# Splitting w_o beside the last products instead of in the chunk stage, in a pool + SSD decoder step

## The chip, the core and the metric

One core of one Trainium2 chip. The metric is the device time of one launch in microseconds; lower is better. The engines are TensorE (PE, with its weight loads PEld), VectorE (DVE), ScalarE (ACT), GpSimd (POOL) and SyncE (SP, which here issues most of the DMAs; ACT issues the rest).

## The reference

One layer of a hybrid decoder, for 1024 prompt rows and 8 x 8 sample rows, in float32:

```
h = rmsnorm(x) * (1 + scale) + shift
[u_pool | z_pool | z_ssm | xBC | dt | g] = h @ w_in
P = (pool_mix(u_pool) * silu(z_pool)) @ w_pool_out
S = gated_rmsnorm(SSD(conv(xBC)) + D*x, z_ssm) @ w_ssm_out
m = sigmoid(g_pool) * P + sigmoid(g_ssm) * S
x = x + gate * (m @ w_o)          # w_o is 1024 x 1024
y = rmsnorm(x)
```

The SSD part is a scan over 8 chunks of 128 rows, for 4 groups of 8 heads. The outputs also hold the new states.

## The kernel before

Every float32 product is made of three matmuls: each operand is split into a part "hi" (a copy in a rounded format, written by ACT) and a part "lo" (value less hi, written by POOL or DVE), and hi*hi, hi*lo and lo*hi are added up in PSUM.

The stages, by the time of the profiled execution: norms and the projections by `w_in` up to about 800 us; the chunk stage (32 chunks, group by group) to about 1120 us; the last products of group 2 to 1140 us; the tail, which is the S products of group 3 with everything that makes m from them, to about 1206 us; and the final product m @ w_o with the last norm to 1297 us.

**Chunk stage.** The loop over the 32 chunks interleaves them with pieces of products (`products(t)`): the eight P units and the S units of groups 0 to 2. PE's order is the order of the code (`in_line((PE,))`). A scheduler sets the order on the other engines, and each engine then works in its order. From chunk 13 on the loop also takes two steps of `wo_splits()` per chunk. For each of 16 half row blocks of w_o (128 x 512) it loads the raw values into `pw` (L1668, SP's queue, two buffers), copies hi into `ph` on ACT (L1674, one buffer), stores hi to the DRAM tile `wo_d` from ACT's queue (L1675), subtracts lo on POOL (L1676), and stores lo from SP's queue (L1670). The steps of a chunk that the prediction speaks of: ACT computes dec (L1196), cE (L1392), bt (L1406), xw (L1415); DVE computes dec (L1416), cE (L1418), xwl (L1419) and the gate product v (L1362); PE uses them in L1208, L1211 and L1429.

**Tail.** `tail_unit(m)` for m = 0 to 7 is one S product (36 matmuls at L354 to L356 in three groups of 384, 352 and 352 columns, into a PSUM pool of three banks) and what follows it. `m_done(m)` loads the gates R (L1785) and the other half of m (L1790), makes the gains R * rstd at the unit's start (L1788, three DVE instructions out of PSUM), adds each group from PSUM to the accumulator G (L1795, DVE), multiplies by R (L1800, DVE) and adds the other half (L1801, POOL, on DVE for m = 7). `wo_prep(k)` loads hi and lo of row block k of w_o back from `wo_d` (L1761, L1762; 512 KB each). `m_split(k)` splits the accumulator: 64 sample columns as `sh` (ACT L1768, DVE L1769), 1024 prompt columns as hi and lo (ACT L1779, DVE L1780). `samples[k]` are four matmuls with the sample columns (L1774). rstd, a row of PSUM that all units use, is made by L1740 to L1749 at the start of the tail. The row blocks 5 to 7 are loaded after the units.

The final product (L1892 to L1894) needs hi and lo of all eight row blocks of w_o and of m for each block of rows.

Of the kernel before, what the change touches and what calls it, by code (L numbers as in the profile page):

```python
# [8 lines left out]
F32 = mybir.dt.float32  # L9
F32R = mybir.dt.float32r  # L10
AF = mybir.ActivationFunctionType
ALU = mybir.AluOpType
# [3 lines left out]
PRIO = 2000  # L16
# [4 lines left out]
P = 128  # L21
D = 1024
# [4 lines left out]
T = SEQ + NS  # L27
# [19 lines left out]
def tile_pool_ssd_step(  # L47
# [6 lines left out]
    nc = tc.nc  # L54
    uid = [0]

    def nm(s):
        uid[0] += 1
        return f"{s}_{uid[0]}"
# [3 lines left out]
    sm = ctx.enter_context(tc.tile_pool(name="sm", bufs=2))  # L63
# [32 lines left out]
    def PB():  # L96
        return psB.tile([P, 512], F32, tag="ps", name=nm("ps"))
# [7 lines left out]
    load = nc.sync.dma_start  # L105
    store_ = nc.scalar.dma_start
    mm = nc.tensor.matmul
    act = nc.scalar.activation
    V = nc.vector
# [77 lines left out]
    dg = []  # L187
# [146 lines left out]
    def in_line(engines, begin=False):  # L334
        traced = nc.cur_bb.bb.instructions
        for i in traced[len(traced) if begin else line[0]:]:
            if i.engine in engines:
                if i.engine in line[1]:
                    tc.add_manual_dep(i, line[1][i.engine], mybir.DependencyInfo(
                        mybir.DependencyClass.NoSync, mybir.DependencyReason.DATA), reason="in_line")  # L340
                line[1][i.engine] = i.name
        line[0] = len(traced)
# [42 lines left out]
    def dram(name, shape, dt=F32):  # L385
        return dr.tile(list(shape), dt, tag=name, name=name)
# [1084 lines left out]
    def run_units(units, ahead=1, beside=None):  # L1471
        pend = {}
        widx = [i for i, u in enumerate(units) if u[0] is not None]
        nxt = 0
        done_w = 0
        for i, (pf, run) in enumerate(units):
            if pf is not None:
                while nxt < len(widx) and nxt <= done_w + ahead:
                    pend[widx[nxt]] = units[widx[nxt]][0]()
                    nxt += 1  # L1480
                done_w += 1
                it = run(pend.pop(i))
                for _ in it or ():
                    if beside is not None:
                        beside()
            else:
                run(None)
        while later:
            step()
# [113 lines left out]
    ck = right.__enter__()  # L1603
# [54 lines left out]
                nxt += 1  # L1658
            yield from run(ws.pop(i))
    pc_ = pieces()  # L1660
    wo_d = [dram(f"wo{k}", [P, 2, D]) for k in range(8)]

    def wo_splits():
        raws = {}
        for n in range(18):
            if n < 16:
                raws[n] = ck.tile([P, 512], F32, tag="pw", name=nm("pw"), bufs=2)
                load(raws[n], w_o[0, n // 2 * P:n // 2 * P + P, n % 2 * 512:n % 2 * 512 + 512])  # L1668
            if n > 1:
                load(wo_d[(n - 2) // 2][:, 1, n % 2 * 512:n % 2 * 512 + 512], raws.pop(n - 2))  # L1670
            yield
            if n < 16:
                hi = ck.tile([P, 512], F32R, tag="ph", name=nm("ph"), bufs=1)
                act(hi, raws[n], AF.Copy)  # L1674
                store_(wo_d[n // 2][:, 0, n % 2 * 512:n % 2 * 512 + 512], hi.bitcast(F32))  # L1675
                nc.gpsimd.tensor_tensor(raws[n].bitcast(F32R), raws[n], hi.bitcast(F32), ALU.subtract)  # L1676
            yield
    wos = wo_splits()
    RATE = 2.56
    FRONT = 4  # L1680

# [11 lines left out]
        next(pc_)  # L1693
    next(seq[0])
    for i in range(len(seq)):
        if i > 12:
            next(wos, None)
        if i + 1 < len(seq):
            with behind(mybir.EngineType.DVE, 1 - i) if i < 2 else ExitStack():
                next(seq[i + 1])  # L1700
        products(i + 0.4)
        if i > 0:
            next(seq[i - 1], None)
        if i > 12:
            next(wos, None)
        next(seq[i], None)
        if i % NC == 3:
            sample_end(i // NC)
        if i + 3 < len(seq):
            next(seq[i + 3])  # L1710
        if i + 2 < len(seq):
            with behind(mybir.EngineType.Activation) if i == 0 else ExitStack():
                next(seq[i + 2])
        products(i + 1.0)
    next(seq[-1], None)
    for it in (pc_, wos):
        for _ in it:
            pass
    in_line((mybir.EngineType.PE,))
    right.__exit__(None, None, None)  # L1720
    while right_all:
# [2 lines left out]


    mp = ctx.enter_context(tc.tile_pool(name="mp", bufs=8, side="right", reuse_waits="tile"))
    mq = open_("mq", 5)

    def M(shape=(P, T), dt=F32):
        return mq.tile(list(shape), dt, tag="m", name=nm("m"))  # L1730
# [6 lines left out]
    ps = PB()  # L1737
    for c in range(9):
        n = min(P, T - c * P)
        mm(ps[:n, c:c + 1], sq_acc[:, c * P:c * P + n], ones[:, 0:1], start=True, stop=True)  # L1740
    for n, c in ((P, slice(0, 8)), (NS, slice(8, 9))):
        act(rs9[:n, c], ps[:n, c], AF.Sqrt, bias=eps[:n], scale=1.0 / DI)
        V.reciprocal(rs9[:n, c], rs9[:n, c])
    rstd = [PB() for _ in range(3)]
    for c in range(9):
        n = min(P, T - c * P)
        dg = sm.tile([P, P], F32, tag="stc", name=nm("dg"), bufs=4)[:n, :n]
        V.tensor_scalar(dg, ident[:n, :n], rs9[:n, c:c + 1], None, ALU.mult)
        mm(rstd[c // 4][:, c % 4 * P:c % 4 * P + n], ones[:n, :], dg, start=True, stop=True)  # L1749

    wo, mh, ml = [None] * 8, [None] * 8, [None] * 8
    w4 = [Y4(hp), Y4(hp)]
    pso = [PB(), PB()]
    samples = []

    def wo_prep(k, mem):
        if k < 4:
            hi, lo = w4[0][:, k, :D], w4[1][:, k, :D]
        else:
            hi, lo = mem((P, D), F32R), mem((P, D), F32R)  # L1760
        load(hi.bitcast(F32), wo_d[k][:, 0])  # L1761
        load(lo.bitcast(F32), wo_d[k][:, 1])  # L1762
        wo[k] = (hi, lo)

    def m_split(k, mem):

        sh = sm.tile([P, P], F32R, tag="stc", name=nm("sh"), bufs=4)
        act(sh[:, 0:NS], acc[k][:, SEQ:], AF.Copy)  # L1768
        V.tensor_tensor(sh[:, NS:P], acc[k][:, SEQ:], sh[:, 0:NS].bitcast(F32), ALU.subtract)  # L1769

        def sample_mm():
            for part in wo[k]:
                for half in range(2):
                    mm(pso[half], sh, part[:, half * 512:half * 512 + 512],  # L1774
                       start=(k == 0 and part is wo[k][0]), stop=(k == 7 and part is wo[k][1]))
        samples.append(sample_mm)
        hi, lo = mem((P, SEQ), F32R), mem((P, SEQ), F32R)
        for o, n in (((0, 384), (384, 384), (768, 256)) if k == 7 else ((0, SEQ),)):
            act(hi[:, o:o + n], acc[k][:, o:o + n], AF.Copy)  # L1779
            V.tensor_tensor(lo[:, o:o + n], acc[k][:, o:o + n], hi[:, o:o + n].bitcast(F32), ALU.subtract)  # L1780
        mh[k], ml[k] = hi, lo

    def m_done(m):
        r = R()
        load(r, gs_d[m])  # L1785
        for j, ps in enumerate(rstd):
            s = slice(512 * j, min(512 * j + 512, T))
            V.tensor_tensor(r[:, s], ps[:, :s.stop - s.start], r[:, s], ALU.mult)  # L1788
        mt = M()
        load(mt, m1_d[m])  # L1790
        a = acc[m]

        def done(o, n, ps):
            s = slice(o, o + n)
            V.tensor_tensor(a[:, s], ps[:, :n], a[:, s], ALU.add)  # L1795
            if m < 7:
                s = slice(0, T)
                if o + n < T:
                    return
            V.tensor_tensor(a[:, s], a[:, s], r[:, s], ALU.mult)  # L1800
            (nc.gpsimd if m < 7 else V).tensor_tensor(a[:, s], a[:, s], mt[:, s], ALU.add)  # L1801
        return done

    def tail_unit(m):
        pf, run_ = S_unit(3, m, m_done)

        def run(w):
            for _ in run_(w):
                pass
            if m < 5:  # L1810
                wo_prep(m, M)
            if m < 7:
                m_split(m, M8 if m < 4 else G)
            if m < 5:
                with tc.high_priority(PRIO):
                    samples[m]()
        return (pf, run)
    run_units([tail_unit(m) for m in range(8)])
    y4 = [Y4(hs), Y4(hs)]
    slots = [y[:, q] for y in y4 for q in range(4)]  # L1820

    def late(shape, dt=F32R):
        return slots.pop(0)[:, :shape[1]]
    for k in (5, 6):
        wo_prep(k, late)
        samples[k]()
    wo_prep(7, late)
    m_split(7, late)
    sample_mm = samples[7]

    def w2k(tag):
# [10 lines left out]
    for half in range(2):  # L1842
        c = slice(half * 512, half * 512 + 512)
# [31 lines left out]
    for i in range(8):  # L1875
# [4 lines left out]
        r = R((P, D))  # L1880
# [6 lines left out]
        for j, (c0, cw) in enumerate(cuts):  # L1887
            s = slice(c0, c0 + cw)
            ps = PB()
# [56 lines left out]
```

## Time and profile before

| | |
|---|---|
| median of 3 runs | 1298.56 us (1297.77 to 1300.59) |
| span of the profiled execution | 1297.1 us |
| PE busy | 1255.9 us, 97% |
| DVE busy | 910.5 us, 70% |
| ACT busy | 708.8 us, 55% |
| POOL busy | 677.4 us, 52% |
| DMA | 251.70 MB, 194 GB/s over the span |

The span is that of one execution under the profiler, of 26554 instructions; the other time is the median of plain runs. PE is the engine with hardly any idle time, so the end moves where PE waits. In a window row the columns are the window, its length, then busy time and number of instructions for PE, PEld, DVE, ACT and POOL, then the granted PE clock, the busy share of the DMA engines and GB/s. In a group row stand busy time, mean ns of one, and the idle time of the engine ahead of them with its releasers. In a row of waits stand who waited for whom, us in total, times, and the longest. In a timeline row stand start, duration, engine and line; in brackets the idle time before it and what ended it.

### The profile page before, as it was taken

The page shows a single profiled execution, that of the slowest core. Times are in us where ns is not written, and L with a number is a line of the kernel's source. Part 1 is how long each engine was busy: PE and PEld are TensorE (multiplying, and loading weights), DVE is VectorE, ACT ScalarE, POOL GpSimd, SP SyncE. Part 2 cuts the span into 40 slices and gives each one's busy share as a digit, 9 for nine tenths or more (in the row PEclk, how much of TensorE's full clock was granted, in tenths as well). Part 3 has the DMA queues.
Part 4 walks back from the last instruction along what each step waited for, and adds up shares of the span by engine and source line. Part 5 has one row for each costly group of instructions (what it writes and reads, how often), then busy time and mean ns, then how long its engine had stood idle before and what let it go on. Part 6 is the DMA issues. An engine that isn't in the chain of part 4 may idle for free.

```text
span 1297.1 us, 26554 instructions
## 1 busy us (share of the span) xinstructions
PE 1255.9 (97%) x9771; PEld 1173.9 (90%) x9771; DVE 910.5 (70%) x1580; ACT 708.8 (55%) x1684; POOL 677.4 (52%) x563
## 2 busy tenths in 40 slices
PE   7999999999999999999999999999998999999998
PEld 6779999989999999999889999889998999999786
DVE  4685778866979578775777665488676888576433
ACT  4665356375656564545455453687987868201111
POOL 1007668677869776664344444276776747314000
PEclk9999999999999999999999999999999999999999
DMA  9837345465455544444656555999988656575631
GB/s 326 259 107 224 119 150 173 142 202 170 146 180 197 165 155 133 161 135 129 181 158 173 152 178 164 356 355 354 338 270 262 202 168 199 172 266 159 226 106 52
DMA packets 233795, 251.70 MB, mean 194 GB/s; under 512 B 31265, under 2 KB 177905, under 8 KB 233658
## 3 DMA queue, kind: packets, MB, share of 16 engines
q1 hardware_dynamic: 161568, 171.60, 42.1%
q10 hardware_dynamic: 72098, 78.41, 17.5%
q8 instruction: 77, 1.26, 0.4%
q14 instruction: 52, 0.43, 0.1%
HBM read 167.06 MB, written 83.01 MB: 193 GB/s over the span
## 4 chain that ended last, share of the span: by engine, by line
PE 67%; issue 8%; DMA 8%; DVE 6%; POOL 5%; ACT 4%; SPq 0%; ACTq 0%; POOLq 0%; DVEq 0%
PE ps L603 6%; PE ps L604 6%; PE ps L605 6%; PE mm L603 6%; PE mm L605 6%; PE mm L604 6%; PE mm L355 3%; PE mm L356 3%; PE mm L354 3%; PE ps L1208 2%; PE ps L1892 2%; PE ps L1894 2%; PE ps L1893 2%; POOL wlo L163 2%; PE ps L1211 2%
## 5 line engine op out<-in xcount | busy, mean ns | idle before, releaser
L163 POOL TENSOR_TENSOR wlo<-rawA,whi 128x512 fp32r<-128x512 f32 x120 | 184.0, 1538 | 185.6 <-ACT whi L160 101.6
L163 POOL TENSOR_TENSOR wlo<-raw,whi 128x512 fp32r<-128x512 f32 x92 | 150.7, 1646 | 125.3 <-ACT whi L160 91.1
L354 PE MATMUL mm<-Y,whi 128*128 128x352 f32 (+1 forms) x480 | 160.1, 334 | 0.7 <-DVE G L1795 0.5
L355 PE MATMUL mm<-Y,whi 128*128 128x352 f32 (+1 forms) x480 | 157.3, 328 | 1.0 <-DVE Y L1466 1.0
L356 PE MATMUL mm<-Y,wlo 128*128 128x352 f32 (+1 forms) x480 | 156.9, 327 | 0.0
L605 PE MATMUL mm<-Y,wlo 128*128 128x272 f32 x496 | 143.6, 290 | 3.9 <-POOL wlo L163 3.1
L603 PE MATMUL ps<-Y,whi 128*128 128x272 f32 x496 | 144.5, 291 | 2.3 <-ACT o L803 1.7
L603 PE MATMUL mm<-Y,whi 128*128 128x272 f32 x496 | 146.5, 295 | 0.2
L604 PE MATMUL ps<-Y,whi 128*128 128x272 f32 x496 | 143.1, 289 | 0.0
L604 PE MATMUL mm<-Y,whi 128*128 128x272 f32 x496 | 142.9, 288 | 0.0
L605 PE MATMUL ps<-Y,wlo 128*128 128x272 f32 x496 | 142.6, 288 | 0.0
L160 ACT ACTIVATE whi<-rawA 128x512 fp32r<-128x512 f32 x125 | 78.2, 626 | 95.6 <-PE ps L604 44.9
L1051 DVE SCALAR_TENSOR_TENSOR GA<-GA,cvT,GA 128x1112 f32<-128x1112 f32 x72 | 127.1, 1769 | 0.6 <-ACT GA L1048 0.5
L160 ACT ACTIVATE whi<-raw 128x512 fp32r<-128x512 f32 x96 | 58.7, 626 | 91.4 <-DVE raw L549 41.7
L605 PEld LDWEIGHTS mm<-Y,wlo 128*128 128x128 f32 x496 | 93.4, 188 | 5.8 <-POOL wlo L163 4.2
L603 PEld LDWEIGHTS ps<-Y,whi 128*128 128x128 f32 x496 | 93.3, 188 | 4.0 <-ACT o L803 1.9
L603 PEld LDWEIGHTS mm<-Y,whi 128*128 128x128 f32 x496 | 93.3, 188 | 2.5 <-issue 0.8
L604 PEld LDWEIGHTS mm<-Y,whi 128*128 128x128 f32 x496 | 93.4, 188 | 0.7 <-issue 0.6
L604 PEld LDWEIGHTS ps<-Y,whi 128*128 128x128 f32 x496 | 93.3, 188 | 0.3 <-issue 0.2
L605 PEld LDWEIGHTS ps<-Y,wlo 128*128 128x128 f32 x496 | 93.4, 188 | 0.2 <-issue 0.2
L354 PEld LDWEIGHTS mm<-Y,whi 128*128 128x128 f32 x480 | 90.3, 188 | 3.2 <-DVE G L1795 1.4
L355 PEld LDWEIGHTS mm<-Y,whi 128*128 128x128 f32 x480 | 90.3, 188 | 3.2 <-DVE Y L1466 1.6
(452 smaller groups left out, 3851.6 us busy)
## 6 DMA issues: line engine op xcount, KB each, us to landing
rawA<-in_w_in SPq DMA_DIRECT2D x46, 512.0 KB
dec<-acs_d SPq DMA_DIRECT2D x32, 512.0 KB
xbc<-GA ACTq DMA_DIRECT2D x24, 512.0 KB
xb<-xbc SPq DMA_DIRECT2D x32, 384.0 KB
rawA<-in_w_in SPq DMA_DIRECT2D x32, 256.0 KB
pw<-in_w_ssm_out ACTq DMA_DIRECT2D x32, 256.0 KB
ws<-ph ACTq DMA_DIRECT2D x32, 256.0 KB
ws<-pw SPq DMA_DIRECT2D x32, 256.0 KB
```

The source lines that it names most:

```text
L160: ins = act(hi[:, :, :ncols], raw[:, :, :ncols], AF.Copy)
L163: (eng or nc.gpsimd).tensor_tensor(lo[:, :, :ncols], raw[:, :, :ncols], hi[:, :, :ncols].bitcast(F32), ALU.subtract)
L354: mm(ps[:, :n], a, rh[k][:, o:o + n], start=(k == 0), stop=False)
L355: mm(ps[:, :n], a, rl[k][:, o:o + n], start=False, stop=False)
L356: mm(ps[:, :n], b, rh[k][:, o:o + n], start=False, stop=(k == nk - 1))
L603: mm(p, hi, ah, start=(k == 0), stop=False)
L604: mm(p, hi, al, start=False, stop=False)
L605: mm(p, lo, ah, start=False, stop=(k == 3))
L1051: V.scalar_tensor_tensor(d[:, :n], rp[:, k:k + n], cvT[:, 24 * k + mc:24 * k + mc + 1], d[:, :n], ALU.mult, ALU.add)
L1208: mm(o[hh], xd[:S, 2 * q + hh, :], dec[:S, 2 * q + hh], start=True, stop=state is None)
L1211: mm(o[hh], state[:, h * 64:h * 64 + 64], cE[:, h], start=False, stop=True)
L1892: mm(ps[:, :cw], mhk, wo[k][0][:, s], start=(k == 0), stop=False)
```

## The change

`wo_splits()` and the DRAM tiles `wo_d` go, with the steps in the chunk loop. In the tail, `wo_load(k)` loads the raw row block k (128 x 1024, 512 KB) into a tile of the pool `mq`, and `wo_split(k)` copies hi on ACT and subtracts lo on POOL (on DVE for k = 7), in the units 0 to 5 and after them for 6 and 7. `mq` has 8 buffers instead of 5, and the nine diagonal tiles `dg` lie in one of them. In unit m the split of m - 1 and the sample matmuls of m - 2 are made. The gains are made behind the unit's adds, except for m = 7. PE and DVE follow the order of the code in the tail. The DMA scratch of the program is set to 1024.

```
-    wo_d = [dram(f"wo{k}", [P, 2, D]) for k in range(8)]
-    def wo_splits(): ...
     for i in range(len(seq)):
-        if i > 12:
-            next(wos, None)
...
-        if i > 12:
-            next(wos, None)
...
-    mq = open_("mq", 5)
+    mq = open_("mq", 8)
...
+    dgs = M()
     for c in range(9):
-        dg = sm.tile([P, P], F32, tag="stc", name=nm("dg"), bufs=4)[:n, :n]
+        dg = dgs[:n, c * P:c * P + n]
...
-    def wo_prep(k, mem):
+    raws = {}
+    def wo_load(k):
+        raws[k] = M((P, D))
+        load(raws[k], w_o[0, k * P:(k + 1) * P, :])
+    def wo_split(k, mem):
         if k < 4:
             hi, lo = w4[0][:, k, :D], w4[1][:, k, :D]
         else:
             hi, lo = mem((P, D), F32R), mem((P, D), F32R)
-        load(hi.bitcast(F32), wo_d[k][:, 0])
-        load(lo.bitcast(F32), wo_d[k][:, 1])
+        raw = raws.pop(k)
+        act(hi, raw, AF.Copy)
+        (V if k == 7 else nc.gpsimd).tensor_tensor(lo, raw, hi.bitcast(F32), ALU.subtract)
         wo[k] = (hi, lo)
...
     def m_done(m):
         r = R()
         load(r, gs_d[m])
-        for j, ps in enumerate(rstd):
-            ...
+        def gains():
+            for j, ps in enumerate(rstd):
+                s = slice(512 * j, min(512 * j + 512, T))
+                V.tensor_tensor(r[:, s], ps[:, :s.stop - s.start], r[:, s], ALU.mult)
+        if m == 7:
+            gains()
...
                 if o + n < T:
                     return
+                gains()
             V.tensor_tensor(a[:, s], a[:, s], r[:, s], ALU.mult)
...
-            if m < 5:
-                wo_prep(m, M)
-            if m < 7:
-                m_split(m, M8 if m < 4 else G)
-            if m < 5:
-                with tc.high_priority(PRIO):
-                    samples[m]()
+            wo_load(m)
+            if m < 6:
+                wo_split(m, M)
+            if m > 0:
+                m_split(m - 1, M8 if m < 5 else G)
+            if m > 1:
+                samples[m - 2]()
+    in_line((mybir.EngineType.PE, mybir.EngineType.DVE), True)
     run_units([tail_unit(m) for m in range(8)])
...
-    for k in (5, 6):
-        wo_prep(k, late)
-        samples[k]()
-    wo_prep(7, late)
+    for k in (6, 7):
+        wo_split(k, late)
+    samples[6]()
     m_split(7, late)
+    in_line((mybir.EngineType.PE, mybir.EngineType.DVE))
...
-    nc = _bacc.Bacc("TRN2", target_bir_lowering=False, num_devices=1)
+    nc = _bacc.Bacc("TRN2", target_bir_lowering=False, num_devices=1, dynamic_dma_scratch_size=1024)
```

The program's order on three engines shows what moves. A row has the line, the operation, output<-inputs and the shape. Line numbers of the kernel after are its own: L1747 is the subtract of `wo_split`, L1790 the add on POOL, L1783 the evictions, L1774 the gains, L1789 the product with R, L1754 and L1765 the subtracts of `m_split`.

ACT before, late in the chunk stage, from the last decay of one chunk to the next gate:

```order
L1196 ACTIVATE dec_13243<-dec_13243,acT 128x128 x8
L1674 ACTIVATE ph_14849<-pw_14803 128x512
L1406 ACTIVATE bt_13285<-ps_13282 128x128
L1415 ACTIVATE xw_13292<-ps_13277 128x512
L1450 ACTIVATE xD_13328<-ps_13323 128x512
L1675 DMA wo_11234<-ph_14849 128x512
L1408 ACTIVATE ps_13282<-xb_13112 128x128
```

and after, at the same place:

```order
L1196 ACTIVATE dec_13216<-dec_13216,acT 128x128 x8
L1406 ACTIVATE bt_13255<-ps_13252 128x128
L1415 ACTIVATE xw_13262<-ps_13247 128x512
L1408 ACTIVATE ps_13252<-xb_13092 128x128
L1450 ACTIVATE xD_13298<-ps_13293 128x512
```

The copy and the store of w_o stood ahead of bt and xw and between them and the next chunk's work; now nothing stands there.

POOL before, from its last instructions for the chunks (L1369, L1370) into the tail:

```order
L1369 TENSOR_TENSOR sz_15040<-sz_15040 128x128
L1370 TENSOR_TENSOR sq_acc<-sq_acc,sz_15040 128x128
L1801 TENSOR_TENSOR G_12288<-G_12288,m_15440 128x1088
L1801 TENSOR_TENSOR G_12415<-G_12415,m_15508 128x1088
L1801 TENSOR_TENSOR G_12570<-G_12570,m_15576 128x1088
L1801 TENSOR_TENSOR G_12696<-G_12696,m_15644 128x1088
```

and after; Y_15295 and Y_15296 hold hi and lo of the row blocks 0 to 3, and the m tiles are the raw rows or, in L1790, the other half of m:

```order
L1370 TENSOR_TENSOR sq_acc<-sq_acc,sz_14920 128x128
L1747 TENSOR_TENSOR Y_15296<-m_15358,Y_15295 128x1024
L1747 TENSOR_TENSOR Y_15296<-m_15417,Y_15295 128x1024
L1790 TENSOR_TENSOR G_12280<-G_12280,m_15309 128x1088
L1747 TENSOR_TENSOR Y_15296<-m_15483,Y_15295 128x1024
L1747 TENSOR_TENSOR Y_15296<-m_15553,Y_15295 128x1024
L1790 TENSOR_TENSOR G_12407<-G_12407,m_15368 128x1088
L1747 TENSOR_TENSOR m_15626<-m_15623,m_15625 128x1024
L1790 TENSOR_TENSOR G_12562<-G_12562,m_15434 128x1088
```

Two subtracts of w_o stand ahead of the first add, two ahead of the second and one ahead of the third.

DVE before, in the unit whose accumulator is G_12883:

```order
L1788 TENSOR_TENSOR R_15777<-ps_15394,R_15777 128x512
L1788 TENSOR_TENSOR R_15777<-ps_15395,R_15777 128x64
L1769 TENSOR_TENSOR sh_15624<-G_12570,sh_15624 128x64
L1800 TENSOR_TENSOR G_12696<-G_12696,R_15639 128x1088
L1780 TENSOR_TENSOR m_2657_15628<-G_12570,m_2656_15627 128x1024
L1795 TENSOR_TENSOR G_12883<-mm_15714,G_12883 128x384
L1795 TENSOR_TENSOR G_12883<-mm_15728,G_12883 128x352
```

and after, a unit in whole:

```order
L1783 TENSOR_TENSOR G_12688<-mm_15506,G_12688 128x384
L1783 TENSOR_TENSOR G_12688<-mm_15520,G_12688 128x352
L1783 TENSOR_TENSOR G_12688<-mm_15534,G_12688 128x352
L1774 TENSOR_TENSOR R_15502<-ps_15273,R_15502 128x512
L1774 TENSOR_TENSOR R_15502<-ps_15274,R_15502 128x512
L1774 TENSOR_TENSOR R_15502<-ps_15275,R_15502 128x64
L1789 TENSOR_TENSOR G_12688<-G_12688,R_15502 128x1088
L1754 TENSOR_TENSOR sh_15557<-G_12562,sh_15557 128x64
L1765 TENSOR_TENSOR m_2628_15561<-G_12562,m_2627_15560 128x1024
```

The gains stood ahead of a unit's evictions and now stand behind them; the product of a unit and the split of the unit before it follow each other behind all three evictions.

More of the change, by code (lines that the diff above doesn't have):

```diff
@@ L1660, in tile_pool_ssd_step @@
     pc_ = pieces()
-    wo_d = [dram(f"wo{k}", [P, 2, D]) for k in range(8)]
[L1663 to L1678, printed above, removed]
     RATE = 2.56
@@ L1715, in tile_pool_ssd_step @@
     next(seq[-1], None)
-    for it in (pc_, wos):
-        for _ in it:
-            pass
+    for _ in pc_:
+        pass
     in_line((mybir.EngineType.PE,))
@@ L1785, in m_done @@
         load(r, gs_d[m])
-        for j, ps in enumerate(rstd):
-            s = slice(512 * j, min(512 * j + 512, T))
-            V.tensor_tensor(r[:, s], ps[:, :s.stop - s.start], r[:, s], ALU.mult)
+        def gains():
[4 more added lines that the diff above has]
+            gains()
         mt = M()
```

## The prediction

> **What bounds the kernel now.** I read the page's busy times, then a table of windows cut at the stage borders, then, for the two stages that the change touches, the waits, the groups by line and the timelines.
>
> ```profile
> PE 1255.9 (97%) x9771; PEld 1173.9 (90%) x9771; DVE 910.5 (70%) x1580; ACT 708.8 (55%) x1684; POOL 677.4 (52%) x563
> core 0: us, PE busy (x) PEld busy (x) DVE busy (x) ACT busy (x) POOL busy (x), PEclk, DMA share, GB/s
> 800.00:840.00 40.00, 37.83 (x288) 36.63 (x288) 16.50 (x34) 25.31 (x53) 15.34 (x11) 1.00 0.95 327
> 840.00:1000.00 160.00, 152.41 (x1253) 140.98 (x1250) 122.70 (x182) 132.74 (x364) 109.49 (x117) 1.00 0.96 320
> 1000.00:1120.00 120.00, 119.63 (x996) 110.99 (x995) 100.75 (x160) 84.86 (x231) 73.42 (x90) 1.00 0.56 169
> 1140.00:1206.00 66.00, 65.34 (x373) 61.51 (x374) 49.60 (x89) 10.36 (x20) 21.05 (x9) 1.00 0.67 221
> ```
>
> PE is busy 97% of the span, and the matmuls of both kernels are the same in number and form. So the change can only take away or add idle time of PE. From 840 to 1000 us, where the w_o pieces run, PE idles 160 - 152.41 = 7.59 us; from 1000 to 1120, in the same chunk loop without them, 0.37 us; in the tail, 1140 to 1206, 0.66 us. The most that the change can bring is therefore about 8 us. The profiled span is 1297.1 us and the median of the runs 1298.56, so 1.5 us lie around the span; I carry differences over unchanged. A measurement of this kernel can tell about 0.2%, that is 2.6 us, from no change.
>
> **The change part by part: the chunk stage.** These groups and waits are those of 840 to 1000 us.
>
> ```profile
> L1676 POOL TENSOR_TENSOR pw<-pw,ph 128x512 fp32r<-128x512 f32 x16 | 22.1, 1379 | 16.4 <-ACT ph L1674 16.4
> L1674 ACT ACTIVATE ph<-pw 128x512 fp32r<-128x512 f32 x16 | 10.0, 626 | 8.5 <-DMA pw<-in_w_o 3.9 <-DMA wo<-ph 3.4 <-POOL sz L1369 1.2
> PE ps L1208 <- DVE dec L1416: 2.3, 2, 1.4
> PE ps L1211 <- DVE cE L1418: 2.3, 3, 0.8
> PE ps L1429 <- DVE xwl L1419: 2.0, 1, 2.0
> PE ps L1211 <- POOL Y L1373: 0.8, 1, 0.8
> 981.30 0.63 ACT L1674 ACTIVATE ph<-pw 128x512 fp32r<-128x512 f32 x1 [2.75 <-DMA wo<-ph]
> 981.83 0.58 ACT L1415 ACTIVATE xw<-ps 128x512 fp32r<-128x512 f32 x1
> 982.45 0.69 DVE L1419 TENSOR_TENSOR xwl<-ps,xw 128x512 fp32r<-128x512 f32 x1 [1.85 <-ACT xw L1415]
> 957.68 1.30 POOL L1676 TENSOR_TENSOR pw<-pw,ph 128x512 fp32r<-128x512 f32 x1
> 957.91 1.63 DVE L1362 TENSOR_TENSOR v<-v,sz 128x512 f32<-128x512 f32 x1
> 979.91 0.68 DVE L1362 TENSOR_TENSOR v<-v,sz 128x512 f32<-128x512 f32 x1
> 847.16 0.63 ACT L1674 ACTIVATE ph<-pw 128x512 fp32r<-128x512 f32 x1 [3.28 <-DMA pw<-in_w_o]
> ```
>
> Removed are 16 copies on ACT (10.0 us) with 8.5 us in which ACT stood before them, 16 subtracts on POOL (22.1 us), and 48 transfers of 256 KB, 12.6 MB. ACT works in order, so what stands behind a waiting L1674 is late. I go through PE's idle time by cause. At 981 us ACT waited 2.75 us for the store to let go of the one ph tile; behind it stood xw, behind that xwl on DVE, behind that PE's 2.0 us and 0.2 beside it: 2.2 us go. At 957.9 DVE's L1362 took 1.63 instead of 0.68 us because it began 0.23 us after POOL's L1676: the 0.8 us that PE then waited for cE go. At 847 the 3.28 us wait left ACT without a gap until dec and cE at 856, where PE waited 1.4 us: most of that goes. The copy that stands ahead of xw in the last chunk before 992 us costs 0.5 us. Together 2.2 + 0.8 + 1.4 + 0.5 = 4.9 us. What stays is the idle time behind cE, which is DVE's own rate (dec and cE follow each other there), about 2.5 us; 800 to 840 us has 2.17 us of idle without any w_o piece. Bounds: 2.2 us if only the plain wait at 981 goes, and 7.1 us if the stage comes to the rate of 1000 to 1120 us (7.59 - 160 x 0.37 / 120). I take **4.8 us**. I exclude a loss here: PE's order is row for row the same, and three engines and the queues only lose work. [...]
>
> **The tail: what it adds.** T0 is 1140.4 us, where L1740 ends and unit 0, the first group-3 product, starts.
>
> ```profile
> L1740 PE MATMUL ps<-ones,sq_acc x18: 165/250/250, 1138.5 to 1140.3; 128*128 128x1 f32 x16, 128*64 128x1 f32 x2
> 1122.99 0.56 DVE L1639 TENSOR_TENSOR G<-mm,G 128x384 f32<-128x384 f32 x1 [1.55 <-PE mm L356]
> 1128.91 0.56 DVE L1639 TENSOR_TENSOR G<-mm,G 128x384 f32<-128x384 f32 x1 [1.55 <-PE mm L356]
> L1749 PE MATMUL ps<-dg,ones x18: 271/275/320, 1144.7 to 1152.5; 128*128 128x128 f32 x16, 64*128 64x64 f32 x2
> 1188.75 1.09 PE L1774 MATMUL ps<-m,sh 128*128 128x512 f32 x4
> 1189.68 0.32 PE L356 MATMUL mm<-Y,wlo 128*128 128x352 f32 x1
> L1795 DVE TENSOR_TENSOR G<-mm,G 128x352 f32<-128x352 f32 (+1 forms) x24 | 12.2, 529 | 3.0 <-PE mm L356 3.0
> L1788 DVE TENSOR_TENSOR R<-ps,R 128x512 f32<-128x512 f32 (+1 forms) x24 | 11.3, 527 | 7.1 <-DMA R<-gs 6.7 <-PE ps L1749 0.4
> 1173.28 0.22 DVE L1769 TENSOR_TENSOR sh<-G,sh 128x64 fp32r<-128x64 f32 x1
> 1173.41 1.28 DVE L1800 TENSOR_TENSOR G<-G,R 128x1088 f32<-128x1088 f32 x1
> L1780 DVE TENSOR_TENSOR m<-G,m 128x1024 fp32r<-128x1024 f32 x4 | 4.9, 1216 | 0.0
> 1158.43 2.53 POOL L1801 TENSOR_TENSOR G<-G,m 128x1088 f32<-128x1088 f32 x1 [1.23 <-DVE G L1800]
> 1158.74 2.30 DVE L1769 TENSOR_TENSOR sh<-G,sh 128x64 fp32r<-128x64 f32 x1
> 1174.78 3.43 POOL L1801 TENSOR_TENSOR G<-G,m 128x1088 f32<-128x1088 f32 x1 [4.00 <-DMA m<-m]
> L1779 ACT ACTIVATE m<-G 128x1024 fp32r<-128x1024 f32 x4 | 4.2, 1044 | 0.0
> 1140.00:1155.00 15.00, 15.00 (x97) 14.68 (x98) 10.01 (x27) 0.41 (x2) 0.34 (x1) 1.00 0.93 345
> ```
>
> A unit of 36 matmuls lasts 5.92 us on PE (from one 384-column eviction to the next), the four sample matmuls 0.93 us (1188.75 to 1189.68). The order puts one set of these behind each unit from unit 2 on: 6.85 us. In the same time DVE has 12.2/8 + 11.3/8 + 1.28 + 0.22 + 1.22 = 5.65 us in written order (three evictions, three gains, the product with the gate, the small and the wide subtract). So DVE has 1.2 us to spare in a unit. The moved gains cost no more than before; placed behind the evictions they no longer hold these up while R is loaded, which is worth at most the tail's 0.66 us.
>
> The tail loads 4.2 MB of raw rows where it loaded 8.4 MB of halves. New are, for each row block of w_o, a copy on ACT (1.04 us; ACT was busy 10.36 of 66 us, so nothing) and a subtract on POOL of 128x1024. No row has it: scaled from L1801 it is 2.53 x 1024 / 1088 = 2.4 us, twice L1676 gives 2.76. I take 2.4, since L1801 is the same kind of instruction in the same stage. Seven of them beside seven adds make 7 x (2.4 + 2.53) = 34.5 us on POOL instead of 20.5, in a tail of some 64 us.
>
> The price is in DVE's waits. At 1158.74 a 64-column subtract that takes 0.22 us took 2.30: it began 0.31 us after POOL's add and ended 0.08 us after it. L1362 above shows the same, and DVE's evictions out of PSUM do not show it. So a DVE instruction with both inputs in SBUF stands until POOL's is done. [...]
>
> With it I lay out the time from T0. Unit 0 contains the 18 rstd matmuls (L1749, 18 x 0.275 us less a little overlap, 4.7 us), so the units end at 10.6, 16.6 and 22.5 us. SP now has the loads of w_o and of m behind the weights of unit 3, which wait for T0; at 345 GB/s, about 1.5 us each, the raw rows land at about 6, 9, 12 and 14.5 us. POOL: subtracts 0 and 1 by 12.6 us, add 0 (behind unit 0's gate product) 13.9 to 16.5, subtract 2 to 18.9. DVE is ready for unit 1's gate product at 18.4, gets in at 18.9 and ends at 20.1. Then subtract 3 runs to 22.5, the small subtract follows, add 1 runs to 25.2, and the wide subtract ends at 26.3. Only behind it stand the evictions of unit 2, whose first group was done at 18.5. PSUM has three slots for these groups, so unit 3, due at 23.4 us, finds none: PE waits about **3.5 us**. From unit 3 on there is one subtract or none in a unit, and DVE catches up, with some 0.3 us of stall. At the end add 6 and subtract 6 stand on POOL in the middle of unit 7's evictions and splits. They put these 2.4 us back and some more through the order of DVE's queue, and the first row block of the final product wants the splits of 6 and 7 only 6 to 8 us after the last unit: **3.3 us**. Sum 7.1 us, less the 0.66 us: **+6.4**. Bounds: 0 if POOL's operations fall into DVE's evictions, and 15 us if the meeting of unit 1 repeats in three units.
>
> Sum: -4.8 + 6.4 = +1.6, on 1298.56: **1300.2 us**.
>
> **The rivals.** A, the sum as it stands, 0.44; its own range is 1297 to 1303.5 (tail 4 to 9, chunks 3 to 6.5).
>
> B, the tail is free. POOL's subtracts run early, before add 0 is due, or DVE's back-to-back instructions keep POOL out, as the 3.43 us of the L1801 at 1174.78, against 2.53, suggest (POOL too is held up). For it: DVE has 1.2 us to spare, unit 0 is long. Then -4.8 and the tail's 0.66 of idle at most: 1298.56 - 4.8 + 0.6 = 1294.4 (without that last 0.6, 1293.8). 0.28. This is the only case clearly faster.
>
> C, a convoy. Each unit's gate product and wide subtract wait for one POOL operation of 2.5 us: DVE's unit is 5.65 + 5.0 = 10.65 against PE's 6.85, 3.8 us lost in each such unit. It decides from the point where DVE waits over 1.2 us in a unit again and again, and ends when POOL has no subtract left; over two units instead of one stall of 3.5, 7.6 us: 1300.2 + 4.1 = 1304.3; over three, 11.4 us: 1308.1. For it: POOL is handed work for units 1 to 4 without a gap. Against it: four of seven subtracts are done by unit 2. 0.20.
>
> D, the chunk stage gives only the 2.2 us of the plain wait, since its other stalls are DVE's own: -2.2 + 6.4 = +4.2, 1302.8. 0.08. That the change doesn't do what it says (w_o there from the start of the tail) is part of A: its loads begin at T0 only, but sample 0 wants row block 0 three units later, at 22.5 us, and it is split at 9.6.
>
> **How the numbers follow.** A is the likeliest: 1300.2 us. Of A I count 0.05 as faster by over 2.6 us, 0.23 within, 0.16 slower; of B 0.23 and 0.05; C all slower; D 0.03 within and 0.05 slower. That makes faster 0.28, same 0.31, slower 0.41. The range goes from B, 1293, to C with two units and a little more, 1306; C with three units and a tail free beside the full 7.1 us are outside.
>
> **What would show it.** Right: PE idles about 2.8 us from 840 to 1000; ACT has no wait over 2 us there but for PE and the decay loads; in the tail PE waits for the eviction ahead of unit 3 and for the splits behind unit 7, some 7 us, and DVE's gate products, small and wide subtracts show 2 to 3.5 us where 0.2 to 1.3 is their own. Wrong: a tail with under 2 us of PE idle (B), waits ahead of three units or more (C), or a chunk stage that idles over 5 us (D).

## The result and the profile after

The kernel after takes 1301.89 us (median of 20 runs, 1297.15 to 1305.49), the kernel before 1298.71 us beside it (20 runs, 1295.12 to 1303.14). The ratio is 1.0024, with a 95% interval of 1.0014 to 1.0034: slower by about 3 us, where the prediction had 1.6 us and a range of 1293 to 1306. The profiled execution has a span of 1301.9 us, 4.8 us more than that of before.

The busy times of the page of after, and the table of windows at the borders that the prediction uses:

```profile
PE 1261.2 (97%) x9771; PEld 1180.0 (91%) x9771; DVE 913.5 (70%) x1581; ACT 709.2 (54%) x1676; POOL 680.1 (52%) x554
800.00:840.00 40.00, 38.96 (x297) 37.53 (x296) 17.79 (x35) 25.08 (x52) 15.06 (x10) 1.00 0.97 334
840.00:1000.00 160.00, 153.24 (x1231) 141.71 (x1230) 117.49 (x179) 124.35 (x346) 88.57 (x101) 0.98 0.75 240
1000.00:1120.00 120.00, 119.87 (x999) 111.25 (x998) 101.36 (x161) 85.22 (x233) 73.28 (x90) 1.00 0.55 168
1140.00:1206.00 66.00, 61.81 (x353) 58.91 (x352) 54.58 (x83) 17.29 (x25) 41.04 (x16) 0.95 0.67 234
```

Two columns matter. PE's idle time from 840 to 1000 us went from 7.59 to 6.76 us only, although DMA's share there fell from 0.96 to 0.75 and ACT and POOL lost 8 and 21 us of work. And the granted clock, 1.00 in all these rows of before, is 0.98 in the chunk stage and 0.95 in the tail: for 6.16 us of the first and 4.51 us of the second PE was busy at a granted clock of 0.50. Its matmuls of 384 columns start 0.32 us apart there (1168.01 and 1168.33 us) and 0.17 us apart at 1.00 (918.74 and 918.91 us).

PE's matmuls come in the same order in both kernels up to the tail, so each can be set against itself. After runs 0.35 us ahead at 800 us and 1.54 us ahead at 840 (a wait of 1.13 us at 838 is gone). It is level at 890 to 910, 3.86 us behind at 915 and 5.97 behind at 930; it makes up for it where before had its own waits, 2.67 behind at 983, and enters the tail 0.52 us behind. It ends 4.8 us behind. The stretch from 800 us to the tail thus cost 0.9 us, and the tail 4.3, counted, here and below, from the first matmul of unit 0 to the last matmul of the kernel.

PE's waits of after, first from 800 to 1120 us, then from 1120 us to the end (who waited for whom, us in total, times, longest):

```profile
PE ps L1208 <- DVE dec L1416: 2.9, 2, 1.7
PE ps L1211 <- DVE cE L1418: 1.9, 3, 0.8
PE mm L355 <- POOL Y L1373: 1.6, 1, 1.6
...
PE mm L354 <- DVE G L1783: 2.3, 1, 2.3
PE ps L1759 <- DVE sh L1754: 1.9, 1, 1.9
```

The 2.0 us for xwl is gone, as forecast. The 1.6 us for POOL's Y is new. Its history in the timeline of after, then two rows for the waits of 1.15 and 0.79 us at 931 us, and last the one row of before that answers to the late cE:

```profile
895.62 1.31 SPq L1182 DMA_DIRECT2D dec<-acs_d  x1
904.15 1.06 ACT L1392 ACTIVATE cE<-dec 128x1024 f32<-128x1024 f32 x1 [5.71 <-DMA dec<-acs_d]
911.84 0.63 ACT L1363 ACTIVATE sz<-v 128x512 f32<-128x512 f32 x1
913.77 1.27 POOL L1373 TENSOR_TENSOR Y<-v,Y 128x512 fp32r<-128x512 f32 x1
915.09 0.66 PE L355 MATMUL mm<-Y,whi 128*128 128x352 f32 x1 [1.62 <-POOL Y L1373]
918.65 0.43 ACTq L1451 DMA_DIRECT2D out<-xD  x1
926.92 1.28 ACT L1423 ACTIVATE xD<-xb,Dv 128x128 f32<-128x128 f32 x4 [4.72 <-DMA out<-xD]
...
905.79 1.04 ACT L1392 ACTIVATE cE<-dec 128x1024 f32<-128x1024 f32 x1
```

ACT stands 5.71 us at cE for a load of decays that took 8.5 us from its issue. Behind it in ACT's queue stand the next gate and the next split, so POOL's lo part comes late and PE waits 1.62 us. In before the scheduler had put other work of ACT ahead of this cE, and it began without a wait.

The waits at 931 us, new as well, have a store behind them. At the end of a group of chunks the state leaves through a tile of the name xD (L1451, issued at 918.65), and ACT then stands 4.72 us at L1423 until that store has landed. xw stands behind it, so DVE's xwl waits 2.02 us for xw, and DVE's dec and cE, for which PE waits, come late. In before ACT had eight decays to compute first and came to this L1423 at 923.75 us without a wait. In the ten traces of kernels without the w_o pieces in the chunk stage (after and experiments 2 to 10), ACT stands 3.8 to 5.6 us for this store, and PE then waits 0.26 to 2.05 us for dec, on the whole more where ACT stood longer; no run took this store away.

The tail, from the timeline of after. The tail starts 0.5 us later here than in before, so T0 is 1140.9 us, and T0 + 26.3 of the prediction is 1167.2:

```profile
1148.60 2.42 POOL L1747 TENSOR_TENSOR Y<-m,Y 128x1024 fp32r<-128x1024 f32 x1 [26.40 <-ACT Y L1746]
1157.36 5.79 POOL L1747 TENSOR_TENSOR Y<-m,Y 128x1024 fp32r<-128x1024 f32 x2
1157.48 3.44 DVE L1789 TENSOR_TENSOR G<-G,R 128x1088 f32<-128x1088 f32 x1
1160.85 2.38 DVE L1754 TENSOR_TENSOR sh<-G,sh 128x64 fp32r<-128x64 f32 x1
1163.16 3.53 DVE L1765 TENSOR_TENSOR m<-G,m 128x1024 fp32r<-128x1024 f32 x1
1163.38 1.51 PE L1759 MATMUL ps<-Y,sh 128*128 128x512 f32 x4 [1.87 <-DVE sh L1754]
1166.61 1.41 DVE L1783 TENSOR_TENSOR G<-mm,G 128x384 f32<-128x384 f32 x3
1167.21 0.69 PE L354 MATMUL mm<-Y,whi 128*128 128x384 f32 x1 [2.32 <-DVE G L1783]
```

The product, the small and the wide subtract of unit 1 each stand for one operation of POOL (3.44, 2.38 and 3.53 us instead of 1.28, 0.22 and 1.22), the evictions begin at 1166.61, and PE waits in two pieces, 1.87 and 2.32 us, ahead of unit 3. Nothing behind it waits.

### The profile page after: what moved, and what is told of

Same layout as the page of the kernel before. It is cut to its first block, busy times and chain, and to the rows that moved or that the text cites. A ratio compares the mean times of both kernels' runs of the same rounds, so it can differ in the third digit from the quotient of the medians.

```text
span 1301.9 us, 26433 instructions
## 1 busy us (share of the span) xinstructions
PE 1261.2 (97%) x9771; PEld 1180.0 (91%) x9771; DVE 913.5 (70%) x1581; ACT 709.2 (54%) x1676; POOL 680.1 (52%) x554
## 4 chain that ended last, share of the span: by engine, by line
PE 80%; DVE 5%; DMA 4%; issue 4%; POOL 3%; ACT 3%; ACTq 0%; SPq 0%; POOLq 0%; DVEq 0%
PE ps L603 7%; PE ps L604 6%; PE ps L605 6%; PE mm L603 6%; PE mm L605 6%; PE mm L604 6%; PE mm L355 6%; PE mm L354 6%; PE mm L356 6%; PE ps L1208 3%; PE ps L1882 2%; PE ps L1884 2%; PE ps L1883 2%; PE ps L1211 2%; POOL wlo L163 2%
```

## The experiments

The theory after the result: the tail's loss is POOL's subtracts of w_o in DVE's way; the chunk stage's missing gain is another order of ACT's work together with late decay loads. The rival for the tail was that the late loads or the pinned order of PE and DVE are to blame, for the chunk stage that its stalls are DVE's own rate or that no gain was there to have.

**1. The tail's change alone.** The w_o pieces are put back in the chunk stage; nothing reads what they store.

```
+    wo_d = [dram(f"wo{k}", [P, 2, D]) for k in range(8)]
+    def wo_splits():
...
+        if i > 12:
+            next(wos, None)
```

> The new tail with the old chunk stage: the sixteen w_o pieces are loaded, split and stored in the chunk stage as before, but nobody reads the stores. Theory 1 (from the two traces: the chunk part nets nothing, about +0.9 us, and the tail part costs 4.4 us): 4 us over before, ratio 1.003, chunk-stage idle of PE back at about 7.6 us, tail idle 4 to 5 us. Rival (the terms of the prediction: chunk -4.8, tail +6.4): 6.4 us over before, ratio 1.005, and 4.8 us over the kernel after. If both parts interact, anything else.

Measured: ratio 1.0101 (1.0074 to 1.0129), 15 us of loss in its profile, 9 of them in the chunk stage. PE's waits of this kernel from 840 to 1000 us and in the tail:

```profile
PE ps L1208 <- DVE dec L1416: 12.1, 3, 5.4
...
PE mm L354 <- DVE G L1806: 2.7, 1, 2.7
```

It isn't the control that it was meant to be: with the pieces back, the scheduler made a third order, in which PE waits 4.53 and 5.37 us for decays at 839.6 and 862.0 us. The tail of this execution, +4.9 us, is near after's +4.3.

**2. The chunk stage's change alone.** Before without `wo_splits()`; the tail loads as many bytes of other weights in the place of w_o.

```
-    wos = wo_splits()
...
-        if i > 12:
-            next(wos, None)
...
-        load(hi.bitcast(F32), wo_d[k][:, 0])
-        load(lo.bitcast(F32), wo_d[k][:, 1])
+        load(hi.bitcast(F32), ws_d[0][k].rearrange("p a b c -> p (a b c)"))
+        load(lo.bitcast(F32), ws_d[1][k].rearrange("p a b c -> p (a b c)"))
```

> The kernel before without the w_o pieces in the chunk stage; its tail loads the same number of bytes in the same form from other split weights, so the final product uses wrong numbers for w_o. Theory 1: the stalls of the chunk stage only move; within 1 us of before, ratio 0.999 to 1.001. Rival (the prediction's term): 4.8 us less than before, ratio 0.9963.

Measured: 1296.51 us, ratio 0.998 (0.9963 to 0.9996). The window row:

```profile
840.00:1000.00 160.00, 156.37 (x1270) 144.69 (x1268) 120.81 (x186) 126.67 (x350) 90.53 (x103) 0.99 0.78 247
```

PE idles 3.63 us here instead of 6.76, with the same work taken away; from 800 us to the tail it gains 2.1 us on before, even with a clock of 0.99. The scheduler ordered ACT differently: ahead of the product at 856 us it put 8 decays instead of 16, and the wait there is 0.28 us instead of 1.75.

**3. The tail without POOL's subtracts.** ACT makes a second copy where POOL subtracted, so lo of w_o is a copy of the raw rows for k < 7.

```
-        (V if k == 7 else nc.gpsimd).tensor_tensor(lo, raw, hi.bitcast(F32), ALU.subtract)
+        if k == 7:
+            V.tensor_tensor(lo, raw, hi.bitcast(F32), ALU.subtract)
+        else:
+            act(lo, raw, AF.Copy)
```

> The kernel after, with POOL's subtracts of w_o left out for the row blocks 0 to 6: lo is a second copy of the raw rows by ACT, so lo of w_o is wrong. Loads, order and matmuls stay. Theory 1 (DVE stands behind POOL's subtracts): DVE's gate products and subtracts return to 1.3, 0.2 and 1.2 us in units 0 to 2, the two waits of PE at 21 us after the start of the tail go, with them the low clock: 4 to 6 us less than after, about 1296.5. Rival (the raw rows land too late, or the written order of DVE is what delays): the waits stay, 1301.9.

Measured: 1294.42 us, ratio 0.9959 (0.9943 to 0.9975).

```profile
1140.00:1206.00 66.00, 66.00 (x376) 62.51 (x375) 47.37 (x85) 24.41 (x33) 24.68 (x9) 1.00 0.76 264
```

PE has no idle time in this window, and the tail is 2.6 us shorter than before's: the loads, the copies and the new order cost nothing, and POOL's subtracts cost 6.9 us in after's tail.

**4. The raw rows earlier.** Rows 0 to 3 are loaded ahead of the tail and split at its start, by POOL as in after. The lines left out put ACT's copies of these four rows behind its other work.

```
+        (store_ if k < 4 else load)(raws[k], w_o[0, k * P:(k + 1) * P, :])
+    for k in range(4):
+        wo_load(k)
...
+    for k in range(4):
+        wo_split(k, M)
     in_line((mybir.EngineType.PE, mybir.EngineType.DVE), True)
```

> The kernel after, with the raw rows 0 to 3 loaded from ACT's queue some 20 us ahead of the tail, and their four splits at the head of the tail, so that POOL subtracts before the first gate product. Theory 1: the four subtracts run from 2 to 11.5 us after the tail's start, where DVE has no instruction with two SBUF inputs; the waits of PE in units 2 and 3 go, 4 to 5 us less than after, about 1297. Rival (the price is in the number of POOL instructions, not their place): under 1.5 us less.

Measured: 1302.13 us, ratio 1.0025 (1.0008 to 1.0043): the stall moved and stayed as large. DVE and POOL at the start of the tail, PE's waits there, and DVE's row of after for the same nine instructions:

```profile
1139.88 10.30 DVE L1733 TENSOR_SCALAR m<-ident,rs 128x128 f32<-128x128 f32 x9
1140.79 9.35 POOL L1749 TENSOR_TENSOR Y<-m,Y 128x1024 fp32r<-128x1024 f32 x4 [20.33 <-DMA wlo<-ws]
PE ps L1734 <- DVE m L1733: 4.3, 3, 1.8
...
1141.69 1.81 DVE L1726 TENSOR_SCALAR m<-ident,rs 128x128 f32<-128x128 f32 x9
```

The rows are there early and the loss remains (+4.6 us in the tail), so it isn't the loads. Four subtracts of POOL now hold up the nine scalings of the identity, 10.30 us instead of 1.81.

**5. All subtracts on DVE**, where the code has them, behind the gate product.

```
-        (V if k == 7 else nc.gpsimd).tensor_tensor(lo, raw, hi.bitcast(F32), ALU.subtract)
+        V.tensor_tensor(lo, raw, hi.bitcast(F32), ALU.subtract)
```

> The kernel after, with the subtracts of w_o on DVE for all row blocks, in the written order behind the gate product of the unit. POOL keeps only the seven adds. Theory 1 (the price of the tail is DVE standing behind POOL's subtracts): one more 1.2 us instruction in each of DVE's units, 5.65 + 1.22 = 6.9 us by the rows against PE's 6.85, and by what overlaps at the instructions' ends rather 6.3: PE waits 0 to 2 us in the tail, 4 to 6 us less than after, 1296 to 1298. Rival (DVE has no room for it: it becomes the bound of the units): DVE late by over 1 us in every unit from unit 3 on, PE waits 5 us or more, no gain over after.

Measured: 1305.58 us, ratio 1.0036 (1.0015 to 1.0057), the tail +7 us. One unit of DVE with POOL's add, and PE's waits in the tail:

```profile
1157.60 1.29 DVE L1789 TENSOR_TENSOR G<-G,R 128x1088 f32<-128x1088 f32 x1
1158.81 1.22 DVE L1747 TENSOR_TENSOR Y<-m,Y 128x1024 fp32r<-128x1024 f32 x1
1158.97 3.43 POOL L1790 TENSOR_TENSOR G<-G,m 128x1088 f32<-128x1088 f32 x1 [2.47 <-DMA whi<-ws]
1159.94 2.54 DVE L1754 TENSOR_TENSOR sh<-G,sh 128x64 fp32r<-128x64 f32 x1
PE ps L1759 <- DVE sh L1754: 4.8, 5, 1.0
PE mm L354 <- DVE G L1783: 2.1, 5, 0.5
```

The product releases POOL's add (the row names a DMA, but the add needs the product's G and begins 0.08 us behind it); it stands while DVE subtracts (3.43 us, against 2.53 at 1158.43 us in before), and behind that the small subtract stands, 2.54 us instead of 0.22. This repeats in five units, in each of which PE waits 1.3 to 1.5 us: a convoy, as rival C has it, made by the place of the subtract and not by its engine.

**6. A fourth buffer for the decays**, so that their loads are issued earlier.

```
-        dec = ckt([P, 8, P], "dec", 3)
+        dec = ckt([P, 8, P], "dec", 4)
```

> The kernel after, with four buffers instead of three for the decay tiles of the chunk stage, so that each decay load may start a chunk earlier. Theory 1 (ACT stands 5.7 us at 898 us for a decay load that lands late, everything behind it in ACT's order is late, and PE loses 3.9 us there and some 2 us behind it): the wait of ACT for decay loads falls under 2 us, PE's waits at 911 to 931 us go, 3 to 5 us less than after, about 1298. Rival (the DMA queue is full and an earlier issue lands no earlier where it counts, or the order that the scheduler makes sets the stalls): the sum of PE's idle time from 840 to 1000 us stays at 6 us or more, in other places.

Measured: 1308.33 us, ratio 1.007 (1.0053 to 1.0088). PE's waits from 800 to 1000 us:

```profile
PE ps L1208 <- DVE dec L1416: 6.4, 3, 3.5
```

ACT no longer waits for a decay load, and the wait for POOL's Y at 913 us is gone, which fits the late load as its cause. It doesn't show it alone, because one buffer more gave the scheduler another order again, with a wait of 3.52 us at 838 us, and the stage lost 4.3 us.

**7. Both 5 and 6.**

> Both: subtracts on DVE and four decay buffers. If the two parts are independent, the sum of their gains over after: with theory 1 in both, 8 to 10 us less than after, about 1293, under the kernel before by 5 us. If only the tail's holds, 1297.

Measured: 1309.98 us, ratio 1.0081 (1.0063 to 1.01), with the stalls of both (chunk stage +6.7 us, tail +8.5).

**8. The subtract on DVE ahead of the gate product.** The instructions of experiment 5 in another order; that of k = 6 stays on POOL, and the load is issued at the unit's start.

```
-        (V if k == 7 else nc.gpsimd).tensor_tensor(lo, raw, hi.bitcast(F32), ALU.subtract)
+        (nc.gpsimd if k == 6 else V).tensor_tensor(lo, raw, hi.bitcast(F32), ALU.subtract)
...
                 gains()
+                if m < 6:
+                    wo_split(m, M)
             V.tensor_tensor(a[:, s], a[:, s], r[:, s], ALU.mult)
...
         def run(w):
+            wo_load(m)
             for _ in run_(w):
                 pass
-            wo_load(m)
-            if m < 6:
-                wo_split(m, M)
```

> The kernel after, with the subtracts of the row blocks 0 to 5 on DVE, but ahead of the unit's gate product instead of behind it (6 stays on POOL, 7 on DVE). Theory (POOL's add is released by the gate product and takes the shared way to SBUF as soon as DVE lets go; three DVE instructions in a row behind the product are one too many): subtract, product, small and wide subtract run at 1.2, 1.3, 0.2 and 1.2 us in a row, the small subtract no longer takes 2.5 us, DVE's unit is 6.3 us, PE has no wait of over 0.5 us before the last unit, and the tail takes 6 to 7 us less than that of the kernel after: 1295 to 1297. Rival (DVE is simply full with seven instructions more): PE loses 1.3 us in each of five units as in the kernel with the subtract behind the product: 1305.

Measured: 1296.43 us against 1300.54 of before in the same comparison, ratio 0.9974 (0.9956 to 0.9993). The same unit as under 5, and the window row:

```profile
1157.51 1.22 DVE L1747 TENSOR_TENSOR Y<-m,Y 128x1024 fp32r<-128x1024 f32 x1
1158.64 1.29 DVE L1791 TENSOR_TENSOR G<-G,R 128x1088 f32<-128x1088 f32 x1
1159.84 0.22 DVE L1754 TENSOR_TENSOR sh<-G,sh 128x64 fp32r<-128x64 f32 x1
1159.97 1.22 DVE L1765 TENSOR_TENSOR m<-G,m 128x1024 fp32r<-128x1024 f32 x1
1160.00 3.60 POOL L1792 TENSOR_TENSOR G<-G,m 128x1088 f32<-128x1088 f32 x1 [3.38 <-DVE G L1791]
...
1140.00:1206.00 66.00, 66.00 (x383) 62.98 (x384) 56.06 (x97) 18.53 (x28) 27.22 (x10) 1.00 0.74 251
```

DVE's four instructions run back to back at their own length, POOL's add comes 0.03 us behind the wide subtract and does the waiting, and PE has no idle time in this window. The tail is 2.6 us shorter than before's and 6.9 us shorter than after's, as short as without POOL's subtracts (experiment 3), with DVE busier than in after (56.06 us against 54.58).

**9. After with the chunk stage's order of experiment 2.** ACT, DVE, POOL and SP are held to the order of that kernel (43 of ACT's 608 instructions of the stage move, 17 of DVE's 359); nothing else changes.

```
+    for e_, s_ in PIN.items():
...
+        for p_, q_ in zip(own, own[1:]):
+            tc.add_manual_dep(q_, p_.name, mybir.DependencyInfo(
+                mybir.DependencyClass.NoSync, mybir.DependencyReason.DATA), reason="pin")
```

> The kernel after, with the order of ACT, DVE, POOL and SP in the chunk stage fixed to that of the kernel that left out the w_o pieces alone (43 of 608 places on ACT differ, 17 of 359 on DVE, 12 of 165 on SP, 3 of 225 on POOL); the tail is that of the kernel after. Theory (the gain of the chunk stage was lost to the order that the scheduler made, ACT's above all): drift at 1010 us falls by 3 us to about -2, the waits of 1.75 us at 854 and 1.6 us at 913 shrink to those of the other kernel, 0.3 and 0.7; 1299. Rival (the loads or the run decide, not the order): the waits stay, 1302.

**10. Both 8 and 9.**

> Both: chunk order fixed and subtracts on DVE ahead of the gate product. If the parts are independent, about 1293, 5 to 6 us less than before, ratio 0.9955; if only the tail's holds, 1296.

Measured: 1301.87 us, ratio 1.0016 (1.0002 to 1.0031) for 9, and 1296.04 us, ratio 0.9962 (0.9945 to 0.9979) for 10, the lowest ratio here of the kernels that leave nothing out. The window rows of 9 and of 10:

```profile
840.00:1000.00 160.00, 155.63 (x1263) 144.03 (x1264) 121.40 (x187) 126.41 (x350) 89.26 (x102) 0.99 0.77 245
...
840.00:1000.00 160.00, 157.05 (x1296) 145.80 (x1295) 122.69 (x188) 129.13 (x357) 93.48 (x107) 1.00 0.77 247
```

With this order the wait at 856 us is under 0.3 us in all three profiles (2, 9, 10), where after's order had 1.74 or 1.75 us in five of five (after, 3, 4, 5, 8). The order is the cause of that wait; which of the four engines' orders it is, the pinning of all four can't tell. The wait at 912 us goes with the decay load instead, as ACT's waits of 2, of 9 and of 10 from 800 to 1000 us show:

```profile
ACT cE L1392 <- DMA dec<-acs_d: 6.3, 2, 4.6
...
ACT cE L1393 <- DMA dec<-acs_d: 6.5, 2, 5.8
...
ACT cE L1393 <- DMA dec<-acs_d: 4.3, 2, 3.4
```

With this order, where ACT stood 5.8, 4.6 and 3.4 us for it (9, 2, 10), PE stood 1.61, 0.70 and 0 us. With after's order PE stood 1.61 or 1.62 us in all five traces, for any wait of ACT from 4.8 to 5.7 us, so the two don't grow together throughout. Why the load lands sooner in one execution than in another wasn't tried. In the medians the order alone isn't told apart: the intervals of 9 and of after overlap, and so do those of 10 and 8. Experiment 10's profile is the fastest of its twelve executions (span 1287.4 us), not a typical one, and has its chunk stage 5.4 us shorter than before's, where 9's is 1.7 us shorter.

## Why the prediction was right, and where it was wrong

The net is 1.6 us below the 3.2 us of the medians. That it came so near is partly luck: in the two profiles the chunk stage was missed by 5.7 us (-4.8 forecast, +0.9 measured) and the tail by 2.1 the other way (+6.4 forecast, +4.3 measured). By terms:

| term | forecast | profile |
|---|---|---|
| chunk stage, PE's idle time | -4.8 | -2.2 |
| chunk stage, granted clock | 0 | +3.1 |
| stall ahead of unit 3 | +3.8 | +4.2, and some 2.7 of clock |
| behind unit 7 | +3.3 | 0 |
| rest of the tail | -0.66 | -2.6 |

The idle time of the chunk stage is the sum of the window rows: 2.17 to 1.04, 7.59 to 6.76 and 0.37 to 0.13 us. The 3.1 is half of the 6.16 us in which PE was busy at half speed (3.01 and 3.15, in the window rows of the last section); with it the chunk stage's two rows make the 0.9 us of the matmuls' starts. The -2.6 is experiment 3's tail; 0.85 us of it are two waits of before's tail (0.55 at 1176 and 0.30 at 1207 us), and where the rest comes from is open. The 2.7 is what is left of the 6.9 us when the 4.2 us of idle time are taken off; PE was busy at half speed for 4.51 us there, which makes 2.3 of it.

- **"I exclude a loss here: PE's order is row for row the same, and three engines and the queues only lose work"** is the step that failed. That the others only lose work doesn't keep their order. The wait at 981 us went as forecast, and so did the short ones at 962 and 991 us; the one at 856, which was to go, grew from 1.40 to 1.75 us, and those at 913 (1.62) and 931 us (1.15 and 0.79) are new. The test that the prediction set for D, over 5 us of idle time from 840 to 1000, is met. D's price for the stage, -2.2, is also what the waits add up to, but by chance: D had the other stalls stay as DVE's own, and here some went and others came. The sign that ACT would wait over 2 us for nothing but PE and the decay loads failed too (4.72 us for the store). A gain of 4.8 us is possible: experiment 10's execution has 5.4.
- **The clock** was in no term. Each of the two stalls at 854 and 913 us was followed by 3.4 us at half speed. Over all runs with a clock on record its mean is 0.9965 for before (68 runs) and 0.9937 for after (20 runs); 0.0028 of 1300 us is 3.6 us, about the whole difference of the medians (they go together over these runs; that is no experiment on the clock).
- **The stall ahead of unit 3** was right in place, cause and size. Subtracts of 2.42 us (forecast 2.4), evictions at T0 + 25.7 (forecast 26.3), PE's wait 4.2 us (forecast 3.5 and 0.3). Experiments 3 and 8 confirm the cause from two sides. That DVE's instructions with inputs in SBUF stand for POOL's is what the rows show (the small subtract took 2.38 us beside POOL's and 0.22 in experiment 8); what the two engines share there isn't shown. Rival B, in which POOL's subtracts cost the tail nothing, is what experiment 8 came to by another place of the subtracts: on DVE, ahead of the gate product.
- **The 3.3 us behind unit 7** were a mis-sized term: POOL's last subtract (1204.73 us, 2.56 us long) does hold up DVE (the gate product of 352 columns at 1205.50 us took 2.18 us, the one at 1203.94 us 0.53), but PE had no gap over 0.12 us after the start of unit 3. The splits came in time.
- **Rival C** didn't come in after, since POOL had done four of its seven subtracts by 1163.15 us, as the prediction argued against it, and the other three (at 1165.6, 1176.7 and 1204.7 us) met no DVE instruction that PE then waited for; experiment 5 shows such a convoy, with five stalls of 1.3 to 1.5 us instead of the 3.8 us worked out for one.

## What to carry to other kernels

DVE and POOL instructions with their inputs in SBUF stood for each other in these profiles (on DVE 0.22 us became 2.38, on POOL 2.53 became 3.43), so count them together, and order DVE's so that those which PE waits for stand ahead of or close behind the one that releases POOL (experiment 8, 1296.43 us; experiment 5, with the subtract between them, 1305.58). Taking work off an engine gives a scheduler another order for what remains, so a gain read off one order's waits needs that order to be kept. In this kernel, with PE busy 97% of the span, stalls of some 1.6 us or more were followed in part of the cases by 3.41 us at a clock of 0.50, which costs up to 1.7 us more. The five stalls of 1.3 to 1.5 us in experiment 5's tail cost nothing more in this way; whether it pays to break a long stall into shorter ones wasn't tried.

## What the runs showed of the hardware

**The clock falls on a grid** in these profiles. Between 800 us and the end of the tail, the profiles of all kernels but before and 10 show stretches at half speed (a granted clock of 0.50). They last 3.4 us or twice that, and within one execution they start whole multiples of 3.413 us apart: in after at 856.81, 914.84 and 1164.01 us, that is 58.03 us or 17 periods and 307.20 us or 90 periods from the first. These are windows of after and then of experiment 5, cut on each execution's own grid (behind the window's length stands PE's busy time, third from the end the granted clock):

```profile
853.38:856.80 3.42, 1.29 (x10) 0.76 (x8) 2.53 (x3) 2.71 (x10) 0.95 (x2) 1.00 0.95 296
856.80:860.21 3.41, 3.01 (x28) 2.88 (x28) 0.59 (x3) 0.00 (x0) 0.00 (x0) 0.50 0.52 182
911.41:914.82 3.41, 1.86 (x14) 0.97 (x10) 2.90 (x5) 3.41 (x10) 2.80 (x3) 1.00 0.91 333
914.82:918.24 3.42, 3.15 (x11) 3.15 (x12) 1.68 (x2) 2.67 (x9) 1.63 (x3) 0.50 0.40 105
...
853.29:856.70 3.41, 0.88 (x10) 0.40 (x10) 2.98 (x4) 2.13 (x8) 0.37 (x1) 1.00 0.87 277
856.70:860.11 3.41, 3.41 (x29) 3.06 (x27) 0.84 (x2) 0.41 (x1) 0.00 (x0) 0.50 0.50 168
928.38:931.79 3.41, 1.89 (x11) 1.57 (x10) 1.35 (x2) 3.41 (x11) 1.96 (x2) 1.00 0.02 7
931.79:935.20 3.41, 2.11 (x32) 1.74 (x32) 1.90 (x4) 3.41 (x11) 0.30 (x2) 1.00 0.86 267
```

In this stretch of all profiles, before and 10 included (their grids laid through the drop at their ends), every period at full speed in which PE idled 1.8 us or more was followed by one at half speed, and, with the exception below, none with 1.5 us or less. Between, both occur: the 1.55 us of the third row was followed by half speed, and 1.75 us of before (979.32 to 982.73 us, with most of its wait of 2.05 us) was not, so the limit isn't sharp in these figures. Experiment 5 stood 2.04 us at 930 us and kept its clock, with the border at 931.79 inside the stall; experiment 7 stood 2.05 us for the same matmul within one period, and the next was at half speed. So a stall of this length cost up to 1.7 us more (half of 3.41) or nothing in these profiles, and the two cases differ in where it fell on the grid. The grid lay elsewhere from profile to profile (experiment 1 has a border at 844.31 us, after at 843.16 and 846.57); whether a kernel can place it wasn't tried. Some of the scatter of the runs may come from this; that isn't shown. The exception: in experiments 1, 7 and 9 a drop near the start of the tail came without a stall, each at the end of the period that held all of the one-column matmuls (L1740 of before, 2.05 us); in the other profiles a border divides them, in after at 1140.1 us.

**A DVE instruction with one tensor input stood for POOL too**: the nine scalings of experiment 4, 128x128 in float32, at 10.30 us beside four subtracts of POOL instead of 1.81 us (the longest took 2.45 us, the median 0.29). The prediction had counted instructions with two inputs in SBUF alone.
